# Weight sums in four buffers, quarter sums in place, compressed features copied by two engines: one change to a two-layer decoder trunk

## The chip, the cores and the metric

The kernel runs on one core of one Trainium2 chip. The core has five engines with instruction streams of their own. TensorE (PE) does the matrix products; its weight loads (PEld) have a record of their own. VectorE (DVE), ScalarE (ACT) and GpSimd (POOL) do the rest of the arithmetic, and SyncE (SP) only issues transfers. Transfers are issued into a queue by an engine (SPq is SP's queue, POOLq is POOL's) and carried out by 16 DMA engines. The engines are kept in step by semaphores: an instruction waits until the ones that it needs are through, and each engine takes its instructions strictly in the order of its own stream.

The metric is the device time of one execution, in microseconds (us), as the median of several runs. Less is better.

## The reference

The reference is a trunk of two layers on one sequence of 512 tokens with 1024 features, in float32. Each layer is a "macaron": half a feed-forward block, a mixer, half a feed-forward block. The mixer of the first layer is a short gated convolution, that of the second is native sparse attention (NSA). Each of the six parts has its own normalization, whose scale, shift and gate come from a conditioning vector.

```python
def adaln(x, g, shift, scale):
    return rms_norm(x, g) * (1 + scale[:, None, :]) + shift[:, None, :]

def swiglu(h, w_in, w_out):                     # w_in 1024 x 5632, w_out 2816 x 1024
    g, u = jnp.split(h @ w_in, 2, axis=-1)
    return (jax.nn.silu(g) * u) @ w_out

# in nsa_mixer: the compressed branch
    def compress(t, w1, w2):                    # blocks of 32 tokens, 16 apart, 4 groups of 64
        blocks = kv(t)[:, blk_idx] + cmp_pos[None, None, :, None, :]
        flat = blocks.transpose(0, 3, 1, 2, 4).reshape(bsz, G, n_cmp, CMP_BLOCK * hd)
        return jax.nn.gelu(flat @ w1) @ w2
    k_cmp = rms_norm(compress(kc, cmp_w1[0], cmp_w2[0]), k_gain[0])
    v_cmp = compress(vc, cmp_w1[1], cmp_w2[1])
...
# each layer i
        h = adaln(x, norm_g[i, 0], shift[:, 0], scl[:, 0])
        x = x + HALF * gate[:, 0, None, :] * swiglu(h, ffn_w_in[i, 0], ffn_w_out[i, 0])
        h = adaln(x, norm_g[i, 1], shift[:, 1], scl[:, 1])
        y = short_conv_mixer(...) if i == 0 else nsa_mixer(...)
        x = x + gate[:, 1, None, :] * y
        h = adaln(x, norm_g[i, 2], shift[:, 2], scl[:, 2])
        x = x + HALF * gate[:, 2, None, :] * swiglu(h, ffn_w_in[i, 1], ffn_w_out[i, 1])
```

## The kernel before

**Layout and precision.** x stays on chip as eight tiles of 128 features by 512 tokens; the matrix products are made in a reduced float32 format (fp32r). So that they are as exact as float32, every operand is split into a rounded part and a rest, and each product is three matmuls: high by high (L168), weight high by rest (L169), weight rest by high (L170). A weight is split by the helper `split`: ACT copies it to the rounded format (L164), DVE subtracts (L165). The normalized input is split likewise, into `hhi` and `hlo`.

**Stages.** The six parts run one after the other: a feed-forward block `ffn_first`, the convolution, a feed-forward block `ffn` (from about 580 us on), the second layer's `ffn` (from about 950), NSA (from about 1311), and the last `ffn` (from about 1662). The end of each part and the start of the next overlap.

**One `ffn`.** Its 22 pieces j are 128 columns of g and of u each. Pieces 0 and 1 are made by `head_start`, which feeds each tile of h to four products as soon as the tile is normalized. Piece 2 is made by `pair`, two plain products of 512 columns. From piece 3 on, `seven_products` makes the product of a 2 by 2 block matrix with seven block products instead of eight: each is 12 matmuls of 256 columns, over sums of weight quarters (`qa`, `qb`, and the plain weight `raw`) and sums of quarters of h (`th`, `tl`). `Norm.quarters` makes the sums of h: ACT adds the shifts into a copy `hfull` of h, DVE forms t0 to t3, and each is split.

The weight sums of one piece: SP loads two quarters into `qa` (L471, L472), two accumulating loads of POOL's queue add a third quarter to both (L474), SP loads the other half of the weight, `raw` (L475), POOL's queue loads one quarter into `qb[0]` (L476), and DVE makes two further sums in `qb` (L477, L478). Then `raw`, `qa` and `qb` are split. PE's order within a piece is a11, a12 (the plain weight), s3, s1 (from `qa`), a22, s2 (from `qb`), s4. The first product, a11, is copied out of PSUM by ACT as `p1` (L499) before s1 adds to the same half bank; DVE (L505 to L511) puts the products together with it. `keep` splits the piece's activation into `ahi` and `alo`. The 22 pieces are taken in four parts (six, six, six, four), and behind each part the output projection `y` multiplies its pieces with `ffn_out` weights for all eight tiles of x.

**Memory.** `qa` has two buffers, `qb` one; `raw`, `whi` and `wlo` share three buffers each with every other weight. Small tiles come from `tmp`, whose tag "t" has four buffers of 512 columns (sg, af, p1 and others) and whose tag "xr" has two of 256. h lies in eight tiles, `hhi0` to `hhi3` and `hlo0` to `hlo3`, of two feature tiles by 512 tokens each. `hfull` and the sums t0 to t3 lie in pools that live only through the head start and piece 2; t0 to t3 use the memory in which the head start had its own weight buffers.

**What sets the order.** The kernel is written against a tile framework. A planner, with costs of its own for each instruction, writes the order of every engine's stream; work marked `high_priority` (the copy p1, the norm's small steps, among them `dg` at L248) is preferred. Buffers of a tag are handed out in the order of the program, and a tile waits until the former holder of its buffer has been read for the last time.

**NSA's start.** The head start makes the features kc and vc that are to be compressed, four banks `os` of 512 tokens. `compressor` copies them out with 16 ACT instructions of 64 by 256 elements (L820), into an order in which blocks are contiguous, and returns the generator `compress(kv)`: its first step adds the positions and splits (`flr`, `flh`, `fll`, L831), its second makes the first projection `ph` from four weights, its third the second projection and norm. Between such steps (`next(c0)` for k, `next(c1)` for v) the program makes other products of h with `natural`: the first queries, two k, one v. `natural` takes the two halves of its weight through `nsa_in`, the first from the common pool, the second from `nw`, a pool on memory that the head start's weights had held.

```python
                p1 = tmp("p1", HT)
                with tc.high_priority():
                    nc.scalar.activation(p1, oy[:, lo], AF.Copy)
                product(ox[:, lo], a12, nrm.quarter(1, 0))
                product(oy[:, hi], s3, t3)
                product(oy[:, lo], s1, t1)
                product(oz[:, hi], a22, t4)
                product(ox[:, hi], s2, t2)
```

## Time and profile before

| quantity | value |
|---|---|
| median of three runs | 2044.2 us (2040.03 to 2048.62) |
| profiled execution, its own time | 2051.7 us |
| its span in the profile | 2049.9 us |
| mean granted TensorE clock | 0.986 |
| POOL busy | 266.8 us, 13% |
| moved by DMA | 307.38 MB, 150 GB/s on average |
| transfers issued on SP's and on POOL's queue | 37.4% and 11.9% of 16 engines' span |

The profile is one execution, taken by the hardware profiler. The span runs from its first to its last record. Busy time counts arithmetic; issuing a transfer is not counted. A row of the view of groups names the line, the engine, the operation, what is written and what is read ("gu<-hhi,whi"; buffer numbers are left out), the shape, the number of instructions, and after the bar the busy time, the mean of one in ns, and the time in which the engine had stood idle ahead of them with what ended most of it. A row of the view of waits reads "engine, what waited, line <- what ended the wait: sum, number, longest". A row of the timeline has the start and the length of one instruction in us and, in brackets, the wait ahead of it. The granted clock is the share of full speed that PE had in that stretch. "L164" is a line of the kernel, and since helpers record many operations under one line, the names of the tiles tell them apart.

Two things are not plain from the table. The DMA engines have a full first sixth and a lighter rest: in the page's 40 slices they move 292 to 331 GB/s up to 359 us, and between 33 and 171 later. And a matmul of PE reads longer in its row than its share of PE's time, as matmuls are pipelined; the distance between two starts is what one costs.

### The profile page before, as it was taken

How to read it: one execution, taken by the hardware profiler on the slowest of the kernel's cores; microseconds unless marked ns; L12 is line 12 of the kernel's file. 1: busy time of each engine (PE TensorE's matmuls, PEld its weight loads, DVE VectorE, ACT ScalarE, POOL GpSimd, SP SyncE). 2: the span in 40 equal slices, each digit the busy share in tenths (PEclk: the TensorE clock that was granted, in tenths of full speed). 3: DMA queues.
4: the chain of work that ended last, by engine and by line, in shares of the span. 5: the costliest groups of instructions: out<-in, count | busy, mean ns of one | idle time of the engine just before them, and what ended most of it. 6: DMA issues, size and time to landing. Idle time of an engine off the chain costs nothing. (4 is left out here: it accounts for less than half of the span.)

```text
span 2049.9 us, 32209 instructions
## 1 busy us (share of the span) xinstructions
PE 1970.3 (96%) x12500; PEld 1765.1 (86%) x12500; DVE 1486.0 (72%) x2532; ACT 870.1 (42%) x1361; POOL 266.8 (13%) x393
## 2 busy tenths in 40 slices
PE   5999999999998999999999999989999899999999
PEld 4878888888898898999879899989888788898989
DVE  7878888664457686777758677866787877676865
ACT  3322222332234343344434343465777865343532
POOL 0000000100011011110101111001344430111100
PEclk9999999999999999999999999999999999999999
DMA  8888988422235465553546465143211213575642
GB/s 307 292 306 311 331 314 316 146 97 89 82 88 136 122 165 148 147 169 88 143 114 165 140 153 170 43 134 105 53 46 33 78 48 92 134 171 158 161 118 83
DMA packets 110309, 307.38 MB, mean 150 GB/s; under 512 B 14795, under 2 KB 15067, under 8 KB 110156
## 3 DMA queue, kind: packets, MB, share of 16 engines
q1 hardware_dynamic: 88956, 259.86, 37.4%
q0 software_dynamic: 21200, 45.46, 11.9%
q8 instruction: 98, 1.61, 0.3%
q14 instruction: 55, 0.45, 0.1%
HBM read 302.12 MB, written 3.15 MB: 149 GB/s over the span
## 5 line engine op out<-in xcount | busy, mean ns | idle before, releaser
L164 ACT ACTIVATE whi<-wraw 128x1024 fp32r<-128x1024 f32 (+2 forms) x286 | 284.6, 999 | 578.6 <-PE y L169 242.9
L165 DVE TENSOR_TENSOR wlo<-wraw,whi 128x1024 fp32r<-128x1024 f32 (+2 forms) x286 | 329.2, 1154 | 89.4 <-ACT whi L164 86.6
L168 PE MATMUL gu<-hhi,whi 128*128 128x256 f32 (+1 forms) x808 | 265.1, 328 | 1.2 <-ACT whi L164 0.6
L169 PE MATMUL gu<-hlo,whi 128*128 128x256 f32 (+1 forms) x808 | 265.0, 328 | 0.0
L170 PE MATMUL gu<-hhi,wlo 128*128 128x256 f32 (+1 forms) x808 | 262.6, 327 | 1.7 <-DVE wlo L165 1.7
L168 PE MATMUL y<-ahi,whi 128*128 128x512 f32 x587 | 232.2, 398 | 7.1 <-ACT ahi L164 7.0
L169 PE MATMUL y<-alo,whi 128*128 128x512 f32 x587 | 233.9, 399 | 0.7 <-DVE alo L165 0.7
L170 PE MATMUL y<-ahi,wlo 128*128 128x512 f32 x587 | 232.9, 398 | 0.0
L119 DVE CUSTOM_DVE_ANT_0 adaraw<-adaraw,cond 128x1024 f32<-128x1024 f32 x144 | 173.8, 1221 | 25.4 <-DMA adaraw<-in_adaw 23.6
L474 POOL DMA_DIRECT2D qa<-in_ffi x114 | 104.1, 1004 | 647.5 <-DMA qa<-in_ffi 321.5
L168 PEld LDWEIGHTS gu<-hhi,whi 128*128 128x128 f32 x808 | 151.8, 188 | 19.6 <-ACT whi L164 2.5
L170 PEld LDWEIGHTS gu<-hhi,wlo 128*128 128x128 f32 x808 | 151.2, 188 | 17.5 <-DVE wlo L165 2.3
L169 PEld LDWEIGHTS gu<-hlo,whi 128*128 128x128 f32 x808 | 151.7, 188 | 14.9
L164 ACT ACTIVATE qbh<-qb 128x1536 fp32r<-128x1536 f32 x57 | 85.0, 1490 | 157.0 <-PE gu L169 126.4
L168 PEld LDWEIGHTS y<-ahi,whi 128*128 128x128 f32 x587 | 110.5, 189 | 38.6 <-ACT ahi L164 11.5
L541 DVE SCALAR_TENSOR_TENSOR x<-y,mods,x 128x512 f32<-128x512 f32 x72 | 54.0, 750 | 118.1 <-PE y L170 118.1
L168 PE MATMUL gu<-th,qah 128*128 128x256 f32 x456 | 130.6, 286 | 8.5 <-ACT p L499 8.5
L169 PEld LDWEIGHTS y<-alo,whi 128*128 128x128 f32 x587 | 111.3, 190 | 28.4 <-DVE alo L165 2.2
L170 PEld LDWEIGHTS y<-ahi,wlo 128*128 128x128 f32 x587 | 111.5, 190 | 25.9
L168 PE MATMUL gu<-th,qbh 128*128 128x256 f32 x456 | 127.8, 281 | 2.2 <-ACT qbh L164 2.2
L169 PE MATMUL gu<-tl,qah 128*128 128x256 f32 x456 | 129.9, 285 | 0.0
L170 PE MATMUL gu<-th,qal 128*128 128x256 f32 x456 | 129.7, 284 | 0.0
(293 smaller groups left out, 5213.0 us busy)
## 6 DMA issues: line engine op xcount, KB each, us to landing
adaraw<-in_adaw SPq DMA_DIRECT2D x144, 512.0 KB, 5.8
wraw<-in_ffi SPq DMA_DIRECT2D x119, 512.0 KB, 4.4
qa<-in_ffi SPq DMA_DIRECT2D x114, 256.0 KB, 4.1
qa<-in_ffi POOLq DMA_DIRECT2D x114, 256.0 KB, 5.3
wraw<-in_ffo SPq DMA_DIRECT2D x72, 384.0 KB, 4.7
qb<-in_ffi POOLq DMA_DIRECT2D x57, 256.0 KB, 3.7
wraw<-in_cwi SPq DMA_DIRECT2D x24, 512.0 KB, 3.3
wraw<-in_nwi SPq DMA_DIRECT2D x20, 512.0 KB, 4.1
```

Of the source, the lines that this page charges most:

```text
L119: nc.vector.tensor_tensor_reduce(out=raw, in0=raw, in1=cond, scale=1.0, scalar=0.0, op0=ALU.mult, op1=ALU.add, accum_out=m)
L164: nc.scalar.activation(hi, src, AF.Copy)
L165: nc.vector.tensor_tensor(lo, src, hi, ALU.subtract)
L168: nc.tensor.matmul(o, sh, mh, start=first, stop=False)
L169: nc.tensor.matmul(o, sh, ml, start=False, stop=False)
L170: nc.tensor.matmul(o, sl, mh, start=False, stop=last)
L474: nc.gpsimd.dma_start(qa[:, i], quart(1, 0), accum_op=ALU.add)
L541: nc.vector.scalar_tensor_tensor(x[d], o, mod(s, 2, d), x[d], op0=ALU.mult, op1=ALU.add)
```

## The change

It has three groups of edits.

In `ffn`: h is laid out differently (`alloc_seven` in place of `alloc`). The first four feature tiles are held as quarters, one tile for tokens 0 to 255 and one (`hhi1`, `hlo1`) for tokens 256 to 511; the small class `Halves` finds the right one for a slice of columns. So that no product reads across the two, `pair` makes each of its products in two halves of 256 columns. `seven_products` never reads `hhi1` and `hlo1`, so their memory serves as two further `qa` buffers: pieces 3 and 4 take the two of the pool, 5 and 6 the two quarters, 7 and 8 the pool again, and so on. (The plain products of a piece read quarters 0/0, 1/0 and 1/1 of h, the sums come from `hfull`.) `Norm.quarters` makes its sums in place, in the four quarters of `hfull`; `th` and `tl` are taken ahead of the head start.

In the weight sums: the two accumulating loads become one, whose source is the same quarter twice. The quarter loaded into `qb[0]` gets its own tile `a22`, from the tag "t" of `tmp`, loaded by SP instead of POOL's queue; `qb` shrinks to the two sums made by DVE, and the split of three becomes two splits, of a22 and of the two sums. `p1` moves from the tag "t" to the tag "xr".

In NSA: the 16 copies become the first step of `compress(kv)` itself, eight for k and eight for v, and of each eight four are made by DVE and four by ACT. The order of the steps between the products changes: k's copies and split and v's copies are called ahead of the first queries. `natural` takes its second half from `nw` only where it is told so; the first queries take both halves from the common pool.

```diff
+    class Halves:
+        def __init__(self, *t):
+            self.t = t
+
+        def __getitem__(self, i):
+            a, b = i[1].start, i[1].stop
+            return self.t[a // HT][:, a % HT:b - a // HT * HT]
+
...
             return self.hi, self.lo
 
 
-        def alloc_seven(self, tq):
-            self.full = tq.tile([P, KD, T], F32, name="hfull")
-
-        def alloc_sums(self, tt, tq):
-            self.t = [tq.tile([P, KD // 2, HT], F32, name=f"t{j}") for j in range(4)]
+        def alloc_seven(self, hp, tf, tt):
+            n = KD // 2
+            self.hi, self.lo = [
+                [Halves(*[q[:, d] for q in qs]) for d in range(n)] + [rest[:, d] for d in range(n)]
+                for qs, rest in [([hp.tile([P, n, HT], F32R, name=f"{e}{c}", tag=f"{e}{c}") for c in range(2)],
+                                  hp.tile([P, n, T], F32R, name=f"{e}2")) for e in ("hhi", "hlo")]]
+            self.full = tf.tile([P, KD, T], F32, name="hfull")
             self.th = [tt.tile([P, KD // 2, HT], F32R, name=f"th{j}") for j in range(4)]
             self.tl = [tt.tile([P, KD // 2, HT], F32R, name=f"tl{j}") for j in range(4)]
 
...
             n = KD // 2
             b11, b12 = self.full[:, 0:n, 0:HT], self.full[:, 0:n, HT:T]
             b21, b22 = self.full[:, n:KD, 0:HT], self.full[:, n:KD, HT:T]
-            t = self.t
+            t = b11, b22, b12, b21
             nc.vector.tensor_tensor(t[0], b11, b12, ALU.subtract)
             nc.vector.tensor_tensor(t[2], b22, b12, ALU.subtract)
             nc.vector.scalar_tensor_tensor(t[1], t[0], -1.0, b22, op0=ALU.mult, op1=ALU.subtract)
...
             nc.vector.tensor_mul(af, sg, u)
             self.keep(af)
 
-    def pair(f, j, h, own=None):
+    def pair(f, j, h, own=None, halves=False):
         gu = []
         for c in range(2):
             w = ffn_in(f, j, c, own if c else None)
             o = psum("gu")
-            project(o, w, 0, h, [(k, k) for k in range(KD)], True, True)
+            for a, b in HALVES if halves else ((0, T),):
+                project(o[:, a:b], w, 0, h, [(k, k) for k in range(KD)], True, True, a, b)
             gu.append(o)
         return gu
 
...
     def ffn(s, f, nrm, nxt, w0, ahead):
         with ExitStack() as es:
             hp = pool(es, "hp", 1)
-            h = nrm.alloc(hp)
             hid = Hidden(es, 12)
             keep = hid.keep
             nj = 2
...
                 raw = wp.tile([P, 2, QT], F32, name="wraw", tag="wraw", bufs=3)
                 whi = wp.tile([P, 2, QT], F32R, name="whi", tag="whi", bufs=3)
                 wlo = wp.tile([P, 2, QT], F32R, name="wlo", tag="wlo", bufs=3)
-                qa = swa.tile([P, 2, QT], F32, name="qa", bufs=2)
-                qb = swa.tile([P, 3, QT], F32, name="qb")
+                i = (j - nj) % 4
+                qa = (swa.tile([P, 2, QT], F32, name="qa", bufs=2) if i < 2 else
+                      hp.tile([P, 2, QT], F32, name="qa", tag=("hhi1", "hlo1")[i - 2]))
+                a22 = tmp("a22")
+                qb = swa.tile([P, 2, QT], F32, name="qb")
                 ah_, al_ = (sw.tile([P, 2, QT], F32R, name=f"qa{e}", bufs=2) for e in "hl")
                 bh_, bl_ = (sw.tile([P, 3, QT], F32R, name=f"qb{e}") for e in "hl")
                 e = sw.tile([P, 4, HT], F32, name="e")
                 nc.sync.dma_start(qa[:, 0], quart(0, 0))
                 nc.sync.dma_start(qa[:, 1], quart(1, 1))
-                for i in range(2):
-                    nc.gpsimd.dma_start(qa[:, i], quart(1, 0), accum_op=ALU.add)
+                a21 = quart(1, 0)
+                nc.gpsimd.dma_start(qa, bass.AP(tensor=a21.tensor, offset=a21.offset, ap=[a21.ap[0], [0, 2], a21.ap[1]]),
+                                    accum_op=ALU.add)
                 nc.sync.dma_start(raw.rearrange("p a b -> p (a b)"), ffi[f, j, 0].rearrange("p k n -> p (k n)"))
-                nc.gpsimd.dma_start(qb[:, 0], quart(1, 1))
-                nc.vector.tensor_tensor(qb[:, 1], qa[:, 1], raw[:, 0], ALU.add)
-                nc.vector.tensor_tensor(qb[:, 2], qb[:, 1], raw[:, 1], ALU.add)
+                nc.sync.dma_start(a22, quart(1, 1))
+                nc.vector.tensor_tensor(qb[:, 0], qa[:, 1], raw[:, 0], ALU.add)
+                nc.vector.tensor_tensor(qb[:, 1], qb[:, 0], raw[:, 1], ALU.add)
                 split(raw, whi, wlo)
                 split(qa, ah_, al_)
-                split(qb, bh_, bl_)
+                split(a22, bh_[:, 0], bl_[:, 0])
+                split(qb, bh_[:, 1:3], bl_[:, 1:3])
 
                 def product(o, w, b):
                     for i in range(KD // 2):
...
                 ox, oy, oz = psum("gu"), psum("gu"), psum("gu")
                 both = lambda o: o.rearrange("p (a b) -> p a b", a=2)
                 product(oy[:, lo], a11, nrm.quarter(0, 0))
-                p1 = tmp("p1", HT)
+                p1 = tmp("p1", HT, "xr")
                 with tc.high_priority():
                     nc.scalar.activation(p1, oy[:, lo], AF.Copy)
                 product(ox[:, lo], a12, nrm.quarter(1, 0))
...
             js = [(j, c) for j in range(nj) for c in range(2)]
             tt = pool(es, "tt", 1, side="right")
             swa = pool(es, "swa", 1, side="right")
-            with ExitStack() as tq_es:
-                nrm.alloc_seven(pool(tq_es, "tf", 1))
+            with ExitStack() as tf_es:
+                nrm.alloc_seven(hp, pool(tf_es, "tf", 1), tt)
+                h = nrm.hi, nrm.lo
                 with ExitStack() as hw_es:
                     hw = pool(hw_es, "hw", 1)
                     w = w0 + [weights(ffi[f, j, c], KD, P, hw, 1, wp) for j, c in js[len(w0):]]
                     os = head_start(nrm, h, [(lambda k, w=w_: (w, 0, k)) for w_ in w])
-                nrm.alloc_sums(tt, pool(tq_es, "tq", 1))
-                os += pair(f, nj, h)
+                os += pair(f, nj, h, halves=True)
                 nrm.quarters()
             nj += 1
             sw_es = es.enter_context(ExitStack())
...
             qn = [None] * NG
 
 
-            def natural(c, each):
-                w = nsa_in(c, nw)
+            def natural(c, each, own=None):
+                w = nsa_in(c, own)
 
                 def half(hf):
                     o = psum("nat")
...
                 c0, c1 = compress(0), compress(1)
                 vq, vk0, vk1 = squares(), squares(), squares()
                 q0 = natural(0, raw(query_tiles(0), vq))
+                next(c0)
+                next(c0)
+                next(c1)
                 run(q0)
+                normed(qn[0], vq)
+                run(natural(8, raw(kn[0], vk0), nw))
                 next(c0)
-                normed(qn[0], vq)
-                next(c0)
-                run(natural(8, raw(kn[0], vk0)))
                 normed(kn[0], vk0)
                 next(c1)
-                k1 = natural(6, raw(kn[1], vk1))
+                k1 = natural(6, raw(kn[1], vk1), nw)
                 run(k1[:1])
                 next(c0)
                 run(k1[1:])
...
                 next(g)
                 next(c0, None)
                 heads(0, 1)
-                v1 = natural(7, values(vn[1]))
+                v1 = natural(7, values(vn[1]), nw)
                 run(v1[:1])
                 keys(0, 0)
                 next(c1, None)
...
             nc.gpsimd.memset(fll.bitcast(F32), 0.0)
             fhv = flh.rearrange("p i (g n) -> p i g n", g=NG)
             flv = fll.rearrange("p i (g n) -> p i g n", g=NG)
-            t2s = []
-            for kv in range(2):
+
+            def compress(kv):
 
                 t2 = cm.tile([P, NG, 8, 32], F32, name=f"t2{kv}")
                 for A in range(2):
-                    o = os[2 * kv + A]
                     for g in range(2):
-                        ov = o[g * HD:(g + 1) * HD].rearrange("d (m p) -> d p m", p=2)
+                        ov = os[2 * kv + A][g * HD:(g + 1) * HD].rearrange("d (n j p) -> d p n j", p=2, j=8)
                         for e in range(2):
-                            nc.scalar.activation(t2[e * HD:(e + 1) * HD, 2 * A + g].rearrange("p j n -> p n j"),
-                                                 ov[:, e, :].rearrange("d (n j) -> d n j", j=8), AF.Copy)
-                t2s.append(t2)
-
-            def compress(kv):
-                t2 = t2s[kv]
+                            to = t2[e * HD:(e + 1) * HD, 2 * A + g].rearrange("p j n -> p n j")
+                            if e:
+                                nc.vector.tensor_copy(to, ov[:, e])
+                            else:
+                                nc.scalar.activation(to, ov[:, e], AF.Copy)
+                yield
                 for e in range(2):
                     i = slice(8 * e, 8 * e + 8)
                     src = t2[:, :, :, e:e + NCMP].rearrange("p g j n -> p j g n")
```

## The prediction, made before the result was known

> **What bounds the kernel now.** I read four views in this order: the shares by engine, the waits of TensorE (PE) with their owners, busy time and granted clock in stretches around each long wait, and the timelines of the engines named there. PE is the bound:
>
> ```profile
> span 2049.9 us, 32209 instructions
> ...
> PE 1970.3 (96%) x12500; PEld 1765.1 (86%) x12500; DVE 1486.0 (72%) x2532; ACT 870.1 (42%) x1361; POOL 266.8 (13%) x393
> ```
>
> The change removes no matrix product, so it can only win PE time lost in waits or in a low clock. In the waits of PE (sum, times, longest) the rows that the change can reach are these; the last two are the same view cut to one stage, the second and the third of the feed-forward blocks (FFN) that use seven products:
>
> ```profile
> PE gu L168 <- ACT p L499: 8.5, 3, 4.3
> PE ph L168 <- ACT flh L831: 7.3, 1, 7.3
> ...
> PE gu L168 <- ACT qbh L164: 2.2, 3, 0.7
> PE pr L249 <- DVE dg L248: 2.2, 2, 1.9
> PE gu L170 <- DVE wlo L165: 1.7, 3, 0.6
> ```
> ```profile
> PE y L168 <- ACT ahi L164: 3.3, 2, 2.7
> ```
> ```profile
> PE y L168 <- ACT ahi L164: 2.8, 1, 2.8
> ```
>
> The rows for p, qbh and wlo come three times, once in each such FFN: the loss sits at the start of an FFN, while its other pieces run through. In the steady part PE never rests (last row of the next fence: 30.00 of 30 us busy, VectorE (DVE) 24.07). A wait also costs clock afterwards. Columns: length, busy us of PE, PEld, DVE, ACT, POOL, granted clock, DMA share, GB/s:
>
> ```profile
> 601.60:605.01 3.41, 3.41 (x14) 3.23 (x15) 2.69 (x7) 1.65 (x4) 0.00 (x0) 0.50 0.36 62
> 649.38:656.21 6.83, 5.80 (x27) 5.81 (x28) 6.83 (x9) 2.78 (x5) 1.67 (x3) 0.50 0.81 144
> 1007.78:1011.20 3.42, 3.42 (x18) 3.42 (x17) 3.42 (x6) 0.63 (x1) 0.57 (x1) 0.50 0.94 147
> 1035.09:1038.50 3.41, 3.41 (x9) 2.73 (x9) 1.62 (x2) 0.84 (x1) 0.00 (x0) 0.50 0.01 2
> 1345.70:1352.53 6.83, 4.18 (x18) 3.89 (x19) 4.29 (x4) 5.61 (x8) 0.00 (x0) 0.50 0.10 35
> 1745.06:1748.47 3.41, 3.41 (x19) 3.41 (x18) 3.41 (x6) 0.63 (x1) 0.57 (x1) 0.50 1.00 180
> ...
> 1800.00:1830.00 30.00, 30.00 (x260) 30.00 (x259) 24.07 (x30) 14.29 (x17) 5.52 (x7) 1.00 0.59 133
> ```
>
> At a clock of 0.50 half of PE's busy time is lost: 1.7 us in a stretch of 3.41, 2.9 after 649.38, 2.1 after 1345.70. The waits with their low clocks make the pot: A, the copy p1 late, 8.5 + 2.9 + 1.7 + 1.7 = 14.8 us; B, ahi late, 3.3 + 2.8 + 1.7 = 7.8; C, qbh and wlo, 2.2 + 1.7 = 3.9; D, the norm's dg, 2.2 + 1.7 = 3.9; E, compression, 7.3 + 2.1 = 9.4. Together 39.8.
>
> The Trainium skill ("TensorE: Matmul & The Clock Gate", Part 1) has the clock halved after at least one idle window of about 3.4 us. The lengths agree; the cause does not, as waits of at most 2.7 us are followed by 0.50 at 601.60, 1007.78, 1035.09 and 1745.06. By the page's rule those four stretches would cost nothing and the sum below would be near -23 instead of -25; the rows decide.
>
> **The change part by part.**
>
> *Four buffers for weight sums (A, B).* What makes p1 and ahi late is ScalarE's (ACT) order: both stand behind a split of qa that waits for its load. ACT in the second FFN:
>
> ```profile
> 1004.02 1.06 ACT L164 ACTIVATE qah<-qa 128x1024 fp32r<-128x1024 f32 x1 [6.52 <-DMA qa<-in_ffi]
> 1004.99 1.47 ACT L164 ACTIVATE qbh<-qb 128x1536 fp32r<-128x1536 f32 x1
> 1006.36 0.36 ACT L499 ACTIVATE p<-gu 128x256 f32<-128x256 f32 x1
> ```
> ```profile
> 1025.09 1.06 ACT L164 ACTIVATE qah<-qa 128x1024 fp32r<-128x1024 f32 x1 [5.96 <-DMA qa<-in_ffi]
> ```
>
> The third qa of the FFN (j = 5) is loaded late because two buffers exist and it waits for the first:
>
> ```profile
> 993.93 0.33 SPq L471 DMA_DIRECT2D qa<-in_ffi  x1
> ```
>
> After the change j = 5 and 6 go to the quarter of h that is dead once the third pair of projections (j = 2) is through. On PE that is where 512 columns turn into 256:
>
> ```profile
> 989.39 0.39 PE L170 MATMUL gu<-hhi,wlo 128*128 128x512 f32 x1
> 989.62 0.28 PE L168 MATMUL gu<-hhi,whi 128*128 128x256 f32 x1
> 989.74 0.28 PE L169 MATMUL gu<-hlo,whi 128*128 128x256 f32 x1
> ```
>
> So the load can start at 989.6 instead of 993.93, 4.3 us earlier. With 0.4 for the second half's issue, 4.1 to land and 6 for the accumulate (both below) the data are there at 1000.1, not 1004.0; qah, qbh and p1 behind it (1.06 + 1.47 + 0.36) are done at 1003.0. PE had stood from 1006.7, where p1 ended, less its wait of (8.5 - 4.3) / 2 = 2.1: from 1004.6. So the wait is gone by 1.6 us wherever ACT's order has qah. The first FFN's 4.3 are only just covered by the same 4.3, so I keep something back. The load that held ACT to 1025.09 is that of j = 7: it now needs the buffer that j = 5 leaves, after the change the one that j = 3 leaves, two pieces earlier; so B goes too. Late next there is the plain chain from a piece's last product to ahi, which at the later boundaries makes no row among PE's waits. I take A -13 and B -6, bounds 0 and all. The 16 later pieces of each FFN gain nothing: PE is full there.
>
> *One accumulating load, the fourth quarter moved from POOL's queue to SP's.* Median us from issue to landing:
>
> ```profile
> qa<-in_ffi SPq DMA_DIRECT2D x114, 256.0 KB, 4.1
> qa<-in_ffi POOLq DMA_DIRECT2D x114, 256.0 KB, 5.3
> ```
>
> POOL issues 57 of these instead of 114, and an accumulate no longer stands in its queue behind the load of qb[0]. The single one waits for both plain loads and moves 512 KB; the trace has none of that size, so its landing lies between 5.3 us and two in a row, 10.6. I take 6, near the lower end, since the two of today overlap and the bytes are the same; at 10.6 the wait of 2.1 would stay whole. SP gets 57 more issues of 0.33 us, 19 us in all, hidden: SP only issues, up to three pieces ahead. Were that lead gone, each would delay the loads behind it by 0.33.
>
> *a22 (C).* Its tile now shares four buffers with the activation's sg and af, so for the first piece its load comes after six such tiles, where qb's was loaded long before. Behind the four qa loads (about 0.4 us each to issue, 1.6) it lands 4.1 to 6 us later, then a split half of at least 0.63 us: 6.3 to 8.2 us after the pair's end, and PE asks for it after four products of 12 matmuls, 48 x 30/260 = 5.5 us. A wait of 0.8 to 2.7 us at each FFN's start; I take 1.6 and half a low clock, 2.5. Behind it on ACT stand p1 and the next splits, which PE needs 4 us later. Against that C falls away, because the quarter sums move:
>
> ```profile
> 619.47 2.36 DVE L165 TENSOR_TENSOR wlo<-wraw,whi 128x1024 fp32r<-128x1024 f32 x2 [9.22 <-ACT whi L164]
> 621.75 1.22 DVE L310 TENSOR_TENSOR t<-hfull 128x1024 f32<-128x1024 f32 x1
> ```
>
> The sums' tiles lie where the head start's last weight was; in place they need only hfull and can fill the 9.22 us in which DVE stood idle, so wlo and qbh of the first piece no longer queue behind them. Net of C: -3.9 + 3 x 2.5 = +3.6, bounds -3.9 and, with the dearest such wait of the trace at each start (4.3 + 2.9), +17.7.
>
> *Splits in two parts.* qbh and qbl become two instructions each:
>
> ```profile
> L165 DVE TENSOR_TENSOR qbl<-qb,qbh 128x1536 fp32r<-128x1536 f32 x57 | 100.1, 1756 | 10.8 <-ACT qbh L164 10.7
> L165 DVE TENSOR_TENSOR qal<-qa,qah 128x1024 fp32r<-128x1024 f32 x57 | 69.7, 1223 | 44.3 <-ACT qah L164 43.7
> ```
>
> 512 columns more cost 533 ns, so one instruction more costs 1223 - 2 x 533 = 157 ns, 9 us over 57 on DVE, and by 1.06 against 1.49 some 0.2 x 57 = 11 on ACT. Both lie beside PE in the steady part (DVE 24.07 of 30): 0. Were that cover gone, 9 us.
>
> *Half-width pair.* 96 matmuls of 256 columns in place of 48 of 512: by the starts above, 0.12 against 0.23 us apart, 11.5 against 11.0 at worst and, at 30/260 each, 11.1: between 0 and 0.5 per FFN, taken as 0. p1 moves to a tag of two buffers that nothing else uses in an FFN; each serves every second piece: 0.
>
> *dg (D).* In the first FFN the sum into qb stands on DVE ahead of the norm's last steps and waits for the accumulate of qa:
>
> ```profile
> 600.44 0.69 DVE L477 TENSOR_TENSOR qb<-qa,wraw 128x512 f32<-128x512 f32 x1 [2.07 <-DMA qa<-in_ffi]
> ```
>
> On POOL that accumulate stood behind the load of qb[0], which is gone; but the order may put the sum there again, behind a longer accumulate: -2, between 0 and -3.9.
>
> *Compression (E).* ACT makes 16 copies in a row before it gets to anything else:
>
> ```profile
> L820 ACT ACTIVATE t<-hs 64x256 f32<-64x256 f32 x16 | 9.8, 610 | 3.5 <-PE hs L170 3.3
> ```
> ```profile
> 1340.61 0.28 PE L170 MATMUL nat<-whi,hlo 128*128 128x256 f32 x1
> 1348.19 0.58 PE L168 MATMUL ph<-whi,flh 128*128 128x256 f32 x1 [7.30 <-ACT flh L831]
> ```
>
> PE had run out: the second weight of the first projection was in memory held by the head start. Now it is in the common pool, and 96 products (11 us) wait for nothing but it; eight copies go to DVE, and those of v come later. Each projection covers four copies (2.4 us), two splits and an add. Next late may be the compression's four weights, three buffers deep: 1.4 kept back. -8, bounds 0 and -9.4.
>
> Sum: -13 - 6 + 3.6 - 2 - 8 = -25.4. The profiled execution took 2051.7 us (1.8 around its span), so 2026.3; the median of the runs shown, 2044.2, is 7.5 lower: 2019.
>
> **Rivals.** (1) ACT's wait only moves: the order, written from planned landings, finds other work to put behind qah. For it: 6.52 and 5.96 us of such waits today. Against: the bound on p1 above. A, B and D stay, +3.6 and -8 remain: 2040. (2) The whole pot goes and a22 is in time: 2004. (3) Slower: a22 queues on SP behind the activation. If DVE keeps today's order, af of the pair
>
> ```profile
> 994.42 0.68 DVE L393 TENSOR_TENSOR af<-sg,gu 128x512 f32<-128x512 f32 x1
> ```
>
> ends at 995.1 and only then frees a buffer; 6 us of landing and 0.63 of split bring a22 at 1001.7, 6.6 after PE asks (989.6 + 5.5), with 3.4 of low clock 10.0 per FFN; SP's qa loads stand behind it, so A, B, D stay: 30 - 3.9 - 8 = +18, 2062. It decides for slower from 7.4 us per FFN. Against: the idle DVE time above, which lets the activations come early. (4) Compression's gain is lost to its weights' buffers: 2019 + 8 = 2027.
>
> **Numbers.** Forecast 0.50 (own range 2010 to 2030), rival 2 0.13, rival 4 0.10, rival 1 0.17, rival 3 0.10. Half a per cent is 10.2 us, about what a measurement of this kernel tells from no change. Below 2034 lie the forecast, 2 and 4: 0.73; rival 1 is within: 0.17; rival 3 is slower: 0.10. The range takes in rivals 2 and 1: 2004 to 2041.
>
> **What would show it.** Right: no PE wait on p (L499) or flh over 1 us, ACT's waits for qa's DMA near zero, quarter sums within the head start, L820's successor split between ACT and DVE. Wrong: PE waiting for a22's split at each FFN's start, SP held by DVE's af, ACT still waiting for qa, or the reshuffled attention stage losing several us, whose order this change also shifts and which I count as 0.

## The result, and the profile after

The changed kernel takes 2035.8 us (median of 20 runs, 2027.9 to 2043.1) against 2042.6 for the kernel before (20 runs, 2035.9 to 2048.6): a ratio of 0.9969, interval 0.9956 to 0.9981. It is 6 to 7 us faster where 25 were forecast.

The profiled executions differ by more than the medians: 2033.9 us of span against 2049.9. Both kernels scatter over 13 to 15 us, and the execution that the prediction started from, 2051.7, was longer than any of the 20. So I compare stages and waits, not the two spans. The waits of PE in the changed kernel that answer to those of the prediction:

```profile
PE gu L168 <- ACT p L515: 12.3, 3, 7.0
...
PE gu L168 <- ACT whi L164: 4.2, 4, 3.2
...
PE gu L168 <- ACT qbh L164: 2.4, 2, 1.3
...
PE pr L258 <- DVE dg L257: 0.2, 1, 0.2
PE gu L170 <- DVE wlo L165: 0.2, 1, 0.2
PE y L168 <- ACT ahi L164: 0.2, 1, 0.2
```

Gone, or down to 0.2, are flh (E), ahi (B), dg (D) and wlo. The largest, p, has grown from 8.5 to 12.3; the wait for the pair's whi is new. The low clock followed the waits (columns as in the prediction: length, busy us of PE, PEld, DVE, ACT, POOL, granted clock, DMA share, GB/s):

```profile
614.24:617.65 3.41, 3.26 (x13) 2.96 (x14) 3.41 (x5) 3.41 (x5) 0.00 (x0) 0.50 0.28 98
644.96:651.79 6.83, 5.19 (x24) 5.19 (x25) 6.83 (x10) 2.95 (x5) 0.00 (x0) 0.50 0.60 144
996.53:999.95 3.42, 3.42 (x19) 3.42 (x18) 0.00 (x0) 0.00 (x0) 0.00 (x0) 0.50 1.09 302
1726.99:1733.81 6.82, 3.72 (x17) 3.72 (x18) 5.47 (x8) 4.16 (x6) 1.19 (x1) 0.50 0.88 178
```

The four stretches begin in or just behind the waits for whi (which ended at 614.22), p (646.60), qbh (995.31) and, again, p (1730.09). A fifth stretch at 0.50 in these blocks, from 952.16 to 955.57, stands behind a wait of 1.3 us for hhi (it ended at 950.01), at the start of the second `ffn`.

Why p is late shows in the third `ffn`, in the timelines of SP, POOL and ACT of the changed kernel (start, length, what; in brackets the wait ahead):

```profile
1704.79 0.33 SPq L485 DMA_DIRECT2D qa<-in_ffi  x1
1705.16 0.43 SPq L486 DMA_DIRECT2D qa<-in_ffi  x1
1708.46 1.05 SPq L485 DMA_DIRECT2D qa<-in_ffi  x2
1709.57 0.90 SPq L491 DMA_DIRECT2D a<-in_ffi  x2
1710.52 0.42 SPq L486 DMA_DIRECT2D qa<-in_ffi  x1
```
```profile
1709.87 1.20 POOL L488 DMA_DIRECT2D qa<-in_ffi  x1 [43.67 <-DVE qal L165]
1718.69 1.19 POOL L488 DMA_DIRECT2D qa<-in_ffi  x1 [7.62 <-DMA qa<-in_ffi]
```
```profile
1727.25 1.06 ACT L164 ACTIVATE qah<-qa 128x1024 fp32r<-128x1024 f32 x1 [11.18 <-DMA qa<-in_ffi]
...
1729.68 0.36 ACT L515 ACTIVATE p<-gu 128x256 f32<-128x256 f32 x1
```
```profile
1730.09 0.58 PE L168 MATMUL gu<-th,qah 128*128 128x256 f32 x1 [6.99 <-ACT p L515]
```

The two loads at 1704.79 wait for DVE's reading of j = 3's buffer; the two at 1708.46 (L485 twice) wait for PE, for the end of the pair. Which piece a transfer belongs to stands in the built program, where each one names its buffer and its part of the weight. The order that the planner wrote is the same in all three such blocks: POOL's accumulates go j = 3, 4, **7**, 5, 6. Piece 7 has the pool's buffer, which comes free first (SP issues its load at 620.89, 983.56 and 1704.79 in the three blocks), and pieces 5 and 6 have the quarters of h, which come free with the pair (626.27, 986.81, 1708.46). So the transfers of a piece that is needed last go first, three pieces' transfers crowd into one stretch, and j = 5's accumulate, second in the queue, is there at 1727.1. It was not the accumulate of j = 7 that held it: POOL stood idle for 7.62 us ahead of it, until j = 5's own second load had landed. SP had issued that load at 1710.52, behind two loads of a22, and the accumulate could start at 1718.69, 8.2 us later. So j = 5 loses twice, by the later buffer and by slow landings in the crowd. ACT has j = 5's split ahead of j = 4's p, and PE stands 7 us.

Length of the stages in us, worked out from the starts of PE's instructions in the timelines: each `ffn` from the last products of the stage before (the first product written to `ty`; for the second `ffn`, the first to `hs`) to the same mark of the next; "start of NSA" from its first `hs` to its first logits `s`; the last `ffn` up to PE's last product.

| kernel | 1st `ffn` | 2nd | 3rd | sum | start of NSA | median us |
|---|---|---|---|---|---|---|
| before, profile of the prediction | 380.5 | 360.5 | 389.0 | 1130.0 | 100.1 | 2042.6 |
| before, one more profile | 378.2 | 359.4 | 387.6 | 1125.2 | 101.2 | |
| changed | 381.3 | 355.6 | 390.1 | 1127.0 | 90.5 | 2035.8 |
| changed, second execution | 384.1 | 357.7 | 390.1 | 1131.9 | 90.5 | 2034.7 |

The start of NSA gained 9.6 to 10.7. The three `ffn` together gained nothing: 1127 and 1132 against 1130 and 1125. The rest of the kernel scatters from execution to execution (up to the first `ffn` 568.7 to 574.0 in these four).

### The profile page after: what moved, and what is told of

Read it like the earlier page. It is cut to its first block, busy times and chain, and to the rows that moved or that the text cites. A ratio compares the mean times of both kernels' runs of the same rounds, so it can differ in the third digit from the quotient of the medians.

```text
span 2033.9 us, 32445 instructions
## 1 busy us (share of the span) xinstructions
PE 1962.4 (96%) x12644; PEld 1766.0 (87%) x12644; DVE 1494.8 (73%) x2597; ACT 875.3 (43%) x1410; POOL 202.1 (10%) x279
## 4 chain that ended last, share of the span: by engine, by line
PE 83%; DVE 8%; ACT 4%; DMA 2%; issue 2%; SPq 0%; POOL 0%; ACTq 0%; DVEq 0%; POOLq 0%
PE gu L168 13%; PE gu L169 13%; PE gu L170 13%; PE y L168 7%; PE y L169 7%; PE y L170 7%; PE cv L169 2%; PE cv L168 2%; PE hs L168 2%; PE hs L169 2%; PE cv L170 2%; PE hs L170 2%; DVE wlo L165 1%; PE ty L169 1%; PE ty L168 1%
## 5 line engine op out<-in xcount | busy, mean ns | idle before, releaser
L168 PE MATMUL gu<-hhi,whi 128*128 128x256 f32 (+1 forms) x856 | 273.8, 320 | 4.3 <-ACT whi L164 4.2
L169 PE MATMUL gu<-hlo,whi 128*128 128x256 f32 (+1 forms) x856 | 273.8, 320 | 0.0
L170 PE MATMUL gu<-hhi,wlo 128*128 128x256 f32 (+1 forms) x856 | 272.0, 318 | 0.2 <-DVE wlo L165 0.2
L168 PEld LDWEIGHTS gu<-hhi,whi 128*128 128x128 f32 x856 | 161.5, 189 | 19.8 <-ACT whi L164 5.6
L169 PEld LDWEIGHTS gu<-hlo,whi 128*128 128x128 f32 x856 | 161.4, 189 | 13.1
L170 PEld LDWEIGHTS gu<-hhi,wlo 128*128 128x128 f32 x856 | 160.8, 188 | 13.7 <-DVE wlo L165 0.6
L488 POOL DMA_DIRECT2D qa<-in_ffi x57 | 68.6, 1204 | 838.2 <-DVE qal L165 240.1
L168 PE MATMUL gu<-th,qah 128*128 128x256 f32 x456 | 130.1, 285 | 12.3 <-ACT p L515 12.3
L170 PEld LDWEIGHTS y<-ahi,wlo 128*128 128x128 f32 x587 | 110.2, 188 | 25.6
L170 PE MATMUL gu<-th,qbl 128*128 128x256 f32 x456 | 128.4, 282 | 0.7 <-DVE qbl L165 0.7
```

Source lines behind the costliest of these rows:

```text
L168: nc.tensor.matmul(o, sh, mh, start=first, stop=False)
L169: nc.tensor.matmul(o, sh, ml, start=False, stop=False)
L170: nc.tensor.matmul(o, sl, mh, start=False, stop=last)
L488: nc.gpsimd.dma_start(qa, bass.AP(tensor=a21.tensor, offset=a21.offset, ap=[a21.ap[0], [0, 2], a21.ap[1]]), accum_op=ALU.add)
```

## The experiments

**The same two kernels again.** No edit.

> The kernel before, one more profile. If the pot of the prediction (p 8.5, ahi 7.0, qbh 2.2, wlo 1.7, dg 2.2, flh 7.3) belongs to the kernel and not to the one execution of 2051.7 us, each of these rows stands here within 1.5 us, whatever the execution's time; what differs is the low clock and the stretch before the first changed block.

```profile
PE gu L168 <- ACT p L499: 8.4, 3, 3.8
PE ph L168 <- ACT flh L831: 7.3, 1, 7.3
PE y L168 <- ACT ahi L164: 7.1, 5, 2.8
...
PE pr L249 <- DVE dg L248: 2.3, 2, 2.0
PE gu L168 <- ACT qbh L164: 2.2, 3, 0.8
PE gu L170 <- DVE wlo L165: 1.7, 3, 0.6
```

Every row of the pot is there within 0.1 us, in an execution of 2047.0. The waits belong to the kernel. The low clocks behind them do not: half of PE's busy time in them is 8.1 us here against 11.8 before, and behind the waits for dg (2.0) and for the second p (2.5) there is none, as the granted clock is 1.00 from 598 to 604 and from 1003 to 1012.

> The changed kernel once more, unaltered. Theory 1 (the order of the transfers makes the waits): this execution shows the same rows as the first, PE waiting for p (L515) about 12 us in three waits, a wait of about 3 us for whi at the first FFN's start, ahi and flh gone; time about 2036. Theory 2 (the waits are a matter of the single execution): the waits on p differ from 12.3 by more than 4 us, and the total with them.

2034.7 us, ratio 0.9969 (0.9955 to 0.9983). p stood at 17.7 us in three waits, 5.4 more than in the first execution, whi at 4.7; ahi and flh stayed gone. So the places are the order's, as theory 1 had it. But p moved by more than the 4 us that I had set as theory 2's mark, though the median stood still: the size of the wait is partly the execution's. That it hangs on when transfers land is likely, and not shown by this run; the kernel that changes j = 5's buffer, below, decides between the theories.

**The attention stage alone, the feed-forward blocks alone.** The two halves of the diff, each on the kernel before.

> The kernel before with the edits in the attention stage alone (copies by two engines, order of the steps, weights' pool); the feed-forward blocks (FFN) are the old ones. Step E of the prediction: 8 us faster than the kernel before, about 2034.5 against 2042.6, and the wait for flh gone. If this stage gives the whole measured gain of 7, the edits in the FFNs gave nothing or cost 1. Rival: the gain lay in the FFNs, and this kernel is within 2 us of the one before.

2029.8 us, ratio 0.9934 (0.9917 to 0.9951): 10 to 17 us faster. The start of NSA is 91.4 long, and flh is no row of PE's waits any more. That is more than the whole change gained, and more than the 9 to 10 us by which the stage itself is shorter; where the rest comes from was not followed up.

> The changed kernel with the attention stage of before; all edits in the FFNs stay. Theory 1: 0 to 2 us slower than the kernel before (2042.6 to 2044.6), PE waiting for p about 12 us. Rival (the FFNs brought the gain): about 2036.

2044.6 us, ratio 1.0015 (0.9999 to 1.0031); p 13.4, NSA's start 100.8, the three `ffn` 1128.1. The edits in the feed-forward blocks gave nothing or cost a few us.

**Which buffer j = 5 takes.**

```diff
-                i = (j - nj) % 4
+                i = (0, 1, 0, 2, 3)[j - nj] if j - nj < 5 else (1, 0, 2, 3)[(j - nj - 5) % 4]
```

> The changed kernel with one difference: piece j = 5 takes the pool's buffer that j = 3 leaves, as before the change, and j = 6 and 7 take the two quarters of h (from j = 8 on the four go round as in the changed kernel). Theory 1 (the quarters come free only with the pair's end, after the pool's buffer, which j = 7 takes first, so that j = 5's accumulate is second in POOL's queue and lands at 643.6, 1002.3 and 1727.1): now j = 5's accumulate is first, lands near 634.7, 996.8 and 1719.7, and p, 3.1 us behind it, is done before PE asks (641.8, 1004.3, 1722.8). The waits on p fall from 12.3 to under 1 and with their low clock of 0.50 (two stretches of 6.83) the time falls by 12 to 18 us against the changed kernel, to 2018 to 2024. Theory 2 (the transfers are too many at once, whichever is first, and the wait only moves to j = 6's split and the next p): waits on p stay above 8 us and the time within 5 us of the changed kernel.

2017.7 us, ratio 0.988 (0.9861 to 0.9898), with nothing changed but which of the four buffers a piece from j = 5 on takes:

```profile
PE gu L168 <- ACT p L515: 0.9, 1, 0.9
```
```profile
1702.91 1.20 POOL L488 DMA_DIRECT2D qa<-in_ffi  x1 [44.21 <-DVE qal L165]
```
```profile
1713.14 1.06 ACT L164 ACTIVATE qah<-qa 128x1024 fp32r<-128x1024 f32 x1 [5.97 <-DMA a<-in_ffi]
...
1715.58 0.36 ACT L515 ACTIVATE p<-gu 128x256 f32<-128x256 f32 x1
```

ACT's order is the same, j = 5's split still ahead of j = 4's p, but the split now belongs to the first accumulate of the queue (1702.91) and not the second. Theory 1 holds; the three `ffn` take 1112.5.

**Two buffers.** The changed kernel without the quarters of h as buffers.

```diff
-                qa = (swa.tile([P, 2, QT], F32, name="qa", bufs=2) if i < 2 else
-                      hp.tile([P, 2, QT], F32, name="qa", tag=("hhi1", "hlo1")[i - 2]))
+                qa = swa.tile([P, 2, QT], F32, name="qa", bufs=2)
```

> The changed kernel with two qa buffers, those of the pool alone; the two quarters of h are not reused, all other edits stay. Theory 1 (what counts is which buffer j = 5 gets; the early read of j = 3's buffer comes from the sums in place): j = 5's accumulate is first in POOL's queue again, the waits on p fall from 12.3 (17.7 in the second execution) to about 1, as with the pool's buffer first (0.9). What the four buffers are worth is then only the wait for ahi at the end of the first part, 6 with 1.7 of low clock: 2017.7 + 8 = about 2025, some 10 us faster than the changed kernel with four. The prediction's view (the four buffers are what takes p's wait away): with two the waits on p are 8 to 15 and the time is 2036 or more.

2018.7 us, ratio 0.9883 (0.9858 to 0.9908): 17 us faster than with four. No wait for p stands among PE's, and ahi is at 0.4, where I had expected it back. So not even B needed the four buffers; and four of them given out the right way (2017.7) are no faster than two. This kernel still has h in quarters and the pair in halves, so these two are not what cost the time.

**The sums in tiles of their own again**, on the kernel with the pool's buffer first: `t` is allocated behind the head start, as before the change.

```diff
-            t = b11, b22, b12, b21
+            t = self.t
...
+                tq = pool(tf_es, "tq", 1)
+                nrm.t = [tq.tile([P, KD // 2, HT], F32, name=f"t{j}") for j in range(4)]
```

> The kernel with the pool's buffer first, and the quarter sums in tiles of their own behind the head start, as before the change. Theory: the wait for the pair's whi (4.5 us, 3.2 of it in the first FFN, with 1.7 of low clock) goes, as ACT's four splits of the sums no longer stand ahead of it; against it the sums again stand ahead of wlo and qbh (3.9 in the kernel before), and j = 3's buffer is read later, so that j = 5's load starts up to 10 us later against the pair's end and p is late again: waits on p 5 us or more, the time 2022 to 2030. If the sums' place does nothing for p, the time is 2014 to 2019.

2049.7 us, ratio 1.0024 (1.0005 to 1.0043), p 29.6 in three waits, the three `ffn` 1138.4. Worse than I had expected, and 32 us behind the same kernel with the sums in place. The sign was right: it is the place of the sums that makes j = 3's weight sums, and with them its buffer, early. Here the pool's buffer is the late one again. In the third block SP issues the loads into the quarters (j = 7 and 6) 5.3 us ahead of the one into the pool's buffer (j = 5), and j = 5's accumulate goes third, behind those of 6 and 7:

```profile
1719.54 0.80 SPq L485 DMA_DIRECT2D qa<-in_ffi  x2
...
1724.80 0.33 SPq L485 DMA_DIRECT2D qa<-in_ffi  x1
```

**The sums in place, and nothing else**, on the kernel before.

```diff
-        def alloc_sums(self, tt, tq):
-            self.t = [tq.tile([P, KD // 2, HT], F32, name=f"t{j}") for j in range(4)]
...
-            t = self.t
+            t = b11, b22, b12, b21
...
-                nrm.alloc_sums(tt, pool(tq_es, "tq", 1))
```

> The kernel before with one edit: the quarter sums are made in place in hfull, and th and tl are taken ahead of the head start. Two qa buffers, two accumulates, a22 in qb by POOL's queue, the old attention stage. Theory 3 (the sums' place alone moves the weight sums' reads, and with them all loads, ahead of the pair): the waits on p fall from 8.5 to under 2, ahi's from 7.0 to under 2 (1.2 of it lies in the first block), qbh and wlo go; with the low clocks that is up to 14.8 + 7.8 + 3.9 = 26.5 of the prediction's pot, taken as 20: about 2021. Rival (the place helps only with the other edits, as the accumulates of POOL's queue stay in the way): the waits on p stay above 5 and the time is 2030 or more.

2020.2 us, ratio 0.9896 (0.9879 to 0.9912). The lines of PE's waits that are left of A to D:

```profile
PE pr L249 <- DVE dg L248: 2.3, 2, 1.9
PE gu L168 <- ACT p L496: 2.0, 2, 1.6
...
PE gu L168 <- ACT whi L164: 1.2, 4, 0.5
...
PE y L168 <- ACT ahi L164: 0.3, 1, 0.3
```

qbh and the pieces' wlo are no rows any more. The three `ffn` take 1103.2, 22 to 27 less than before. This one edit takes nearly all of A, B and C; p keeps 2.0, and D stays.

**The sums in place and the attention stage.**

> The same with the edits of the attention stage. Theory 3: 9 to 13 us less again, as for those edits alone on the kernel before: 2008 to 2014, and faster than 2018.7 (all edits, two buffers), where ACT's splits of the sums stand ahead of the pair's whi (3.0). Rival (the single accumulate and a22's own load are worth something): 2020 or more.

2011.8 us (2002.7 to 2017.3), ratio 0.9844 (0.9821 to 0.9868): the fastest of all, ahead of both kernels, with p at 0.6 and the three `ffn` at 1099.7. Against the two buffers with all other edits it is 7 us ahead (the intervals of the two ratios just overlap, at 0.9858 to 0.9868); 3.6 of that lie in the first `ffn` (369.7 against 373.3), where the changed kernel's ACT has all four splits of the sums ahead of the pair's weight:

```profile
612.16 1.06 ACT L164 ACTIVATE th<-hfull 128x1024 fp32r<-128x1024 f32 x1 [1.14 <-DVE hfull L324]
613.12 1.99 ACT L164 ACTIVATE whi<-wraw 128x1024 fp32r<-128x1024 f32 x2
```

(These rows are the changed kernel's; PE stands for 3.2 us there, up to 614.22.) In the kernel with the sums in place the two weight splits go ahead of the fourth:

```profile
611.98 2.01 ACT L164 ACTIVATE whi<-wraw 128x1024 fp32r<-128x1024 f32 x2 [1.04 <-PE hs L169]
613.90 1.04 ACT L164 ACTIVATE th<-hfull 128x1024 fp32r<-128x1024 f32 x1
```

The other 3 us are not settled.

**Four buffers on top of that.** h in quarters, the pair in halves and the four buffers as in the change; two accumulates and a22 stay as before.

> The kernel with the sums in place and the new attention stage (2011.8), and on top the four qa buffers as the changed kernel assigns them, with h in quarters and the pair in halves; two accumulates and a22 in qb by POOL's queue stay as before the change. Theory 4 (four buffers by themselves do the harm: j = 7 and j = 6 take the buffers that come free first, and their loads and accumulates stand ahead of j = 5's on SP's and POOL's queues): waits on p of 8 us or more at the FFNs' starts with low clocks behind them, the three FFNs 10 to 25 us longer (1099.7 by the marks of that kernel), the time 2020 to 2037. Rival (the single accumulate's long landing and a22 on SP's queue do the harm): waits on p below 2 and the time within 4 us of 2011.8.

2044.3 us, ratio 1.0012 (0.9995 to 1.0029): 32 us slower than without. p and its low clock:

```profile
PE gu L168 <- ACT p L512: 25.6, 3, 9.2
```
```profile
643.50:653.70 10.20, 4.59 (x21) 4.60 (x22) 8.58 (x11) 4.42 (x6) 0.57 (x1) 0.50 0.37 89
1005.30:1015.50 10.20, 5.09 (x24) 5.09 (x25) 8.57 (x11) 3.93 (x6) 0.57 (x1) 0.50 0.43 98
1732.30:1742.50 10.20, 5.63 (x26) 5.63 (x27) 8.29 (x11) 3.59 (x6) 0.57 (x1) 0.50 0.48 118
```

25.6 of waiting and half of 15.3 busy us are 33. Theory 4 holds: the four buffers, given out in this order, do the harm by themselves, and here the first accumulate of j = 6 went ahead of j = 5's as well.

**Two accumulates; a22 in qb.** Both on the kernel with the pool's buffer first. The first puts back two accumulating loads of 256 KB; the second puts a22 back in a qb of three quarters, split in one, loaded by SP.

> The kernel with the pool's buffer first, and two accumulating loads of 256 KB in place of the one of 512 KB. If the single one's landing (7.1 to 9.9 us at an FFN's start) costs nothing because p's wait is gone: within 3 us of 2017.7. If it is a cost that later waits hide (a22, qbh): 3 us or more faster, with the waits on qbh (3.1) gone.

2022.7 us, ratio 0.9903 (0.9881 to 0.9924). The interval overlaps that of 0.988, so between 0 and some 5 us slower; qbh grew from 3.1 to 4.3, ahi returned with 3.3 and dg with 2.7, and whi fell from 4.5 to 1.9. The single accumulate costs nothing and may be worth a little.

> The kernel with the pool's buffer first, and a22 back in a buffer of three quarters (qb), loaded by SP before the activation's tiles are through, split with the two sums in one instruction. Theory: the wait for a22's split (qbh, 3.1 us in two waits) and the low clock behind it (3.41 at 994.2, and 3.41 of 618.7 in part) go: 3 to 6 us faster, 2012 to 2015. Rival: a single qb buffer brings back the queue on it, waits of 2 us per FFN on qbh or wlo as in the kernel before (2.2 and 1.7): no gain.

2017.5 us, ratio 0.9882 (0.9857 to 0.9906): no gain, where I had expected 3 to 6 us. The wait on qbh is gone, but p is back at 7.8. In all three blocks p stands on ACT behind a step of the piece before (e, L524), which waited 2.2 to 2.5 us for DVE. Why the order came out so was not looked for.

## Why the prediction was wrong

By its steps; the profile before was 2051.7, and its terms are set beside what the stages and waits showed.

- **Four buffers (A -13, B -6): wrong, and the step that failed.** I took the gain of 4.3 us from the second block, where the pair ended at 989.6 and j = 5's load was issued at 993.93. In the kernel before this holds in all three blocks (631.1 and 635.40 in the first, 1726.4 and 1730.68 in the third):

```profile
1726.14 0.39 PE L170 MATMUL gu<-hhi,wlo 128*128 128x512 f32 x1
1726.37 0.28 PE L168 MATMUL gu<-hhi,whi 128*128 128x256 f32 x1
```
```profile
1730.68 0.33 SPq L471 DMA_DIRECT2D qa<-in_ffi  x1
```

  The step that failed is that I held these moments fixed although another edit of the same change moved them. In the second block the sums in place bring DVE's reading of j = 3's buffer from 992.68 to 982.26 (4.0 of it because the block starts earlier, 950.0 against 954.0), ahead of the pair's end:

```profile
992.68 1.23 DVE L165 TENSOR_TENSOR qal<-qa,qah 128x1024 fp32r<-128x1024 f32 x1
```
```profile
982.26 1.23 DVE L165 TENSOR_TENSOR qal<-qa,qah 128x1024 fp32r<-128x1024 f32 x1
```

  (The first row is of before, the second of after.) With that the pool's buffer, which came free 4.3 us behind the pair's end, comes free 5.4, 3.3 and 3.7 us ahead of it in the three blocks: it is the early one, and the quarters are the late ones. So j = 7 overtakes j = 5 on both queues, and p waits 12 to 18 us. Measured for the buffers: +17 (four against two in the changed kernel), +32 (on the kernel with the sums in place), and about 0 where j = 5 gets the buffer that is free first. My sentence that the wait is gone "wherever ACT's order has qah" was about ACT's order; the order that decided was that of SP and POOL.
- **The sums in place: undersized.** I counted them as +3.6 for a22 less 3.9 for C, with dg apart. By themselves they take nearly all of A, B and C: -21 (ratio 0.9896). I had the mechanism in a sentence, the 9.22 us in which DVE stood idle, and did not follow it to the buffer that it frees. The pot of 26.5 for A to C was about right (21 by the medians, 22 to 27 by the three `ffn`); it was put on the wrong edit.
- **The single accumulate:** I took 6 us to land, between 5.3 and 10.6. In the steady part that is right, at the start of a block it is not. It did not decide the time: two accumulates gained nothing on the kernel with the pool's buffer first, and with two the four buffers still cost 32 us. Median us from issue to landing in the changed kernel, for 1704 to 1728 and for 1800 to 1840:

```profile
qa<-in_ffi POOLq DMA_DIRECT2D x4, 512.0 KB, 8.3
```
```profile
qa<-in_ffi POOLq DMA_DIRECT2D x4, 512.0 KB, 5.6
```

- **a22 (+2.5 in each block):** right in kind, smaller in size: in the changed kernel two waits on qbh, of 1.1 and 1.35, and one low clock of 3.42, about 4 us in all against the 7.5 taken.
- **dg (D, -2):** the wait went (2.2 to 0.2; with two accumulates it is back at 2.7, so it is the single one that takes it), and another of 3.2 took its place in the same block, the pair's whi behind the splits of the sums. That I had not seen: I filled DVE's idle time with the sums and did not ask where ACT would put their four splits.
- **Splits in two, half-width pair, p1's tag (0):** nothing shows in a row; not measured apart.
- **Compression (E, -8):** right in its mechanism, a little small in size. 100.1 became 90.5, flh is gone, and by the medians the edits are worth 9 us in the changed kernel (2044.6 without them) and 10 to 17 alone. The weights' buffers, my rival 4, made no row above 0.5.
- **The base:** I set the sum against the median of three, 2044.2; over 20 runs it is 2042.6. Of the miss of 16.8 us this is -1.6; the feed-forward blocks make +14 to +24 (-17.4 forecast, between -3 and +7 by the executions of the table), and E takes back about 2.

The time is nearest to rival 1 (2040), by which the wait on ACT only moves. That agreement is in part luck: I had given ACT's order as its reason, and what moved was the order of the transfers, while B went, D was replaced and the waits behind A grew.

## What to carry to other kernels

Buffers are handed out in the order of the program, and a queue issues in the order in which a planner thinks they come free: more buffers help only if the piece that is needed next gets the one that is free first, and otherwise its transfers stand behind those of later pieces. Before a row is used as the moment at which something comes free, ask whether another part of the same change moves that row, and look at every place where the step occurs, not one. Where a change has several parts on one pot, the experiment with one part alone is cheap: here one edit of a few lines, with the attention stage, gained five times what the whole did (1.56% against 0.31%). And a buffer that is shared with an earlier phase is a hidden order: taking the sums out of the memory of the head start's weights was worth more than any buffer here.

## What the runs showed of the hardware

Transfers landed later in a crowd: the same accumulate of 512 KB took 5.6 us at the median in the steady part, with the core's transfers at 192 GB/s, and 8.3 at the start of a block, at 247 GB/s.

Longer waits mostly had longer low clocks behind them: 3.42 us with a wait for qbh of 1.35, 6.82 and 6.83 with waits for p of 7.0 and 4.5, 10.2 with a wait of 9.2. It is no fixed rule: a wait for p of 7.5 in the kernel with the feed-forward edits alone stands beside 6.83, and the waits of 2.0 and 2.5 named above, in the second profile of the kernel before, had none.

The Trainium skill ("TensorE: Matmul & The Clock Gate", Part 1) has the halved clock begin after at least one idle window of about 3.4 us. Here, as in the prediction's rows, the lengths agree, being near multiples of 3.41; the condition does not, as a stretch also followed a wait of 1.35 us, while longer waits passed without one. The same wait does not always go with the same stretch: the 7.3 us for flh stand beside 6.83 in the profile before, and beside 10.2 in the second profile of the same kernel (1341.78 to 1352.02) and in the kernel with the feed-forward edits alone (granted clock 0.50 from 1338.1 to 1348.3).
